# A seventh gate tile goes from the indexer to the selection, and each counting round hands out a larger share of stream work

## The chip, the cores and the metric

The kernel runs on one core of a Trainium2 chip. The metric is device time in microseconds (us). Three runs of the kernel before gave 1029.61, 1030.85 and 1031.7; the median is 1030.85. The engines are named as the profile names them: PE multiplies matrices (PEld loads its weights), ACT is ScalarE, DVE is VectorE, POOL is GpSimd, and SP issues most of the DMAs. SBUF is the on-chip memory, PSUM the small memory that PE writes its results to.

## The reference

One step of a one-layer encoder: 1024 prompt tokens and 32 sample tokens, model width 1024. A single projection yields everything that the branches need.

```python
h = rms_norm(x, g_norm) * (1.0 + scale) + shift
z = einsum('btd,de->bte', h, w_in)
u, zs, q, k, v, za, qi, ki, wi, gm = split(z, offs)

# indexer and selection
logits = einsum('bthd,bsd->bths', qi, ki) * IDX_DIM ** -0.5
score = einsum('bth,bths->bts', wi, relu(logits))     # -inf where not admissible
top_val, top_idx = top_k(score, n_sel)                # 256 (prompt), 136 (sample)
# attention over the selected keys only, then
ya = o * silu(za)
g_s, g_a = split(gm, 2)
merged = sigmoid(g_s) * (ys @ w_ps) + sigmoid(g_a) * (ya @ w_pa)
out = merged @ w_o
```

The gates gm have 2048 columns: 16 tiles of 128 columns, named g0 to g15 in the kernel. They are needed only at the end of the layer, so the kernel may compute them at any time after h.

## The kernel before

**Tiling.** The 1056 tokens lie in three blocks of 256, 384 and 416 columns (BW). A column tile of the projection is 128 columns of w_in: for each block and each of 8 slices of the model width, `mm3` (lines 271 to 273) issues three matmuls, since every operand is split into a high part and a low part (hH and hL, wh and wl). A tile is 72 matmuls. Its weights are loaded by SP (line 250), cast to wh on ACT (line 259) or POOL (263) and subtracted to wl on DVE or POOL (264). Each block ends with an evacuation of PSUM: for a gate tile a tanh on ACT (line 707); after the third block SP stores the tile (709).

**The stream.** Such tiles are jobs of a stream `Z` (class Stream). The other stages call `run(us)`: this writes as many matmuls of the stream into PE's program as make up that time (by a cost per step of 0.02 + 0.00132 times the block's columns; 11.65 us for a whole tile), between the matmuls of the stage itself. With the second step of a job's first block the next job's weights are split and those of the job after it loaded. With `Z.lag` a block's evacuation is written 4.5 us of handed-out work after its last matmul. PE, ACT and DVE execute in the order in which the program writes (manual schedule); POOL and SP are ordered by the scheduler.

**The stages around the change**, in order:

- The gated linear unit (glu), with qi1, the second pair of indexer heads, behind it in the stream.
- Key preparation: `run(KF)`, the cached keys turned (line 1185), the indexer's keys and weights turned (1194), kiH and kiL split (76 on DVE, 77 on POOL). Also a piece of the output gate (`rpiece`: a 1 MB load of rraw, and matmuls at line 1167).
- The indexer, four pairs of heads. For every pair (j) and every row tile i of 2 to 8, for both heads: score matmuls on PE (lines 1220, 1221), a ReLU on ACT (1223), scaling and sum on DVE (1226, 1228). Behind each, `run(0.25 + nk * FI)` hands out stream work. The score PSUM (pss) has two buffers.
- The selection: 32 counting rounds find each row's threshold bit by bit. In every round ACT counts four row tiles (line 1556), DVE three (1558); then `run(RS)` hands out stream work; then DVE makes the next threshold (1614, 1621). Then the mask stage ("mark"; lines 1628 to 1655), where `run` hands out by the tile's length, 45.2 us in all. Its stream: K, V and Q of the first head pair (K0, V0, Q0), the gate tiles from number NI to 15, four za tiles. In this stage a tile's first two blocks share one PSUM tile (pss, two buffers) and its third has one of another kind (pz, two buffers).
- The attention, with its own stream (K, V and Q of the next heads, then the tiles of w_ps).

The gate tiles are dealt out by two numbers: g0 to g(NS-1) go ahead of the indexer, up to g(NI-1) into the indexer, the rest into the selection.

```python
Z.add(qijob(1), *(gate_job(f, se, ve) for f in range(NS, NI - 1)))          # line 1135
Z.add(qijob(2), qijob(3), gate_job(NI - 1, se, ve), hold=True)
...
for b in range(31, -1, -1):
    ...
    for g in (B1, B2, A):
        g.count()
    run(RS)
    ve.tensor_tensor(keep, cnt, lim, op=ALU.is_ge)
```

qi2 is opened when pair 0 has been written, qi3 and the last gate tile when pair 1 has; so in pair 0 the stream holds what comes ahead of qi2.

Of the kernel before, what the change touches and what calls it, by code (L numbers as in the profile page):

```python
# [25 lines left out]
NCH = 133  # L26
NST = 134
QT = [(i * 128, 128, 128 * (i + 1)) for i in range(8)]
NS, NI = 6, 8
KF = 9.0  # L30
WB = 5
SQ, HF, SM, GD, GH, NP, BL, HB, GL = 1, 4, 4, (1, 1, 0), 1, (0, 0, 2, 2), 1, 1, 0
# [6 lines left out]
TF, TK, TW = 1.5, 1.0, 4.5  # L39
FI = 0.0006  # L40
KA, LA = 5.0, 1.0
LAG, RS, MS, RM, RB = 4.5, 4.1, 0.008, 14.0, 1
FA, FF, SW, SA, SB = ((2.0, 1.3), (2.0, 1.3), (2.4, 1.6), (1.5, 1.5)), 0.08, 1.2, 4.0, 1.0
YR = 3.9, 2.0, 2.0, 8.0, 3.0
MR, ML, YS, YW, HI, HG, JO, SF = (), 1, 10, 15, 0, 0, 8, (2, 2, 2, 1)
# [1876 lines left out]
```

## Time and profile before

| what | value |
|---|---|
| median of three runs | 1030.85 us |
| the profiled execution | 1031.07 us |
| its span, first to last instruction | 1029.3 us |
| busy: PE, PEld | 974.4 us (95%), 904.5 us (88%) |
| busy: DVE, ACT, POOL | 762.7 us (74%), 526.5 us (51%), 233.4 us (23%) |
| mean granted clock of PE | 0.989 |
| chain that ended last | PE 70%, ACT 9%, DVE 8%, DMA 6% |
| DMA, mean over the span | 121 GB/s |

Busy time is the time in which at least one instruction of the engine ran. Of the 40 slices of the page (25.7 us each), the indexer lies in the 12th to 15th, the selection in the 16th to 23rd. A row of the timeline reads: start in us, duration in us (ns in the groups), engine, source line, operation, output<-inputs, shape, and in brackets the engine's idle time ahead of it with the instruction that ended it. A wait for several things is put down to the one that came last by the profile, which can be wrong.

### The profile page before, as it was taken

What the parts mean: (1) busy time and instruction counts of PE and PEld (TensorE: products, weight loads), DVE (VectorE), ACT (ScalarE), POOL (GpSimd) and SP (SyncE); (2) the same over time, 40 slices, a digit from 0 to 9 for tenths busy, and PEclk for the clock granted to TensorE, in tenths of its full rate; (3) what the DMA queues carried; (4) which work ended last, traced back from release to release, by engine and by line L of the source; (5) the groups of instructions that cost most, each with busy time, mean ns of one, the idle gap of its engine ahead of it and who ended that gap; (6) DMA issues with size and microseconds to landing.
All of it is one profiled execution on the core that took longest, in us unless ns stands there. A gap on an engine that the chain in (4) does not pass through costs nothing.

```text
span 1029.3 us, 16904 instructions
## 1 busy us (share of the span) xinstructions
PE 974.4 (95%) x6034; PEld 904.5 (88%) x6034; DVE 762.7 (74%) x1743; ACT 526.5 (51%) x1126; POOL 233.4 (23%) x443
## 2 busy tenths in 40 slices
PE   5999999999999999989998999999999998999997
PEld 3789999999998889889998999999997997998786
DVE  4669899993866879899999758657557685886543
ACT  3642234435546666867994366466465554343111
POOL 3102400000010043333315423334311222530000
PEclk9999999999999999989998999999999999999999
DMA  9922524548483122323313422222416424653411
GB/s 318 277 78 84 147 74 120 128 98 260 134 260 103 40 83 83 93 65 106 102 63 105 136 85 63 88 79 63 132 56 205 131 64 151 209 171 118 133 62 61
DMA packets 134399, 124.24 MB, mean 121 GB/s; under 512 B 20400, under 2 KB 115076, under 8 KB 134316
## 3 DMA queue, kind: packets, MB, share of 16 engines
q1 hardware_dynamic: 133376, 122.62, 38.9%
q8 instruction: 47, 0.77, 0.3%
q10 hardware_dynamic: 780, 0.52, 0.2%
q14 instruction: 36, 0.29, 0.1%
q0 software_dynamic: 160, 0.03, 0.0%
HBM read 87.74 MB, written 34.83 MB: 119 GB/s over the span
## 4 chain that ended last, share of the span: by engine, by line
PE 70%; ACT 9%; DVE 8%; DMA 6%; issue 5%; POOL 1%; SPq 1%; POOLq 0%; ACTq 0%; DVEq 0%
PE pz L271 12%; PE pz L272 11%; PE pz L273 11%; ACT junkb L1556 5%; PE pss L1392 3%; PE psm L1891 3%; PE psm L1892 3%; PE psm L1893 3%; DMA wm<-in_w_mod 2%; PE pt L1485 2%; DVE junk L1558 2%; PE pspo L1504 2%; PE pss L271 2%; PE pss L273 2%; PE pss L272 2%
## 5 line engine op out<-in xcount | busy, mean ns | idle before, releaser
L271 PE MATMUL pz<-hH,wh 128*128 128x384 f32 (+4 forms) x760 | 259.9, 342 | 0.8 <-ACT tg L707 0.5
L272 PE MATMUL pz<-hL,wh 128*128 128x384 f32 (+4 forms) x760 | 250.4, 329 | 0.0
L273 PE MATMUL pz<-hH,wl 128*128 128x384 f32 (+4 forms) x760 | 250.3, 329 | 0.0
L264 POOL TENSOR_TENSOR wl<-raw,wh 128x256 fp32r<-128x256 f32 (+1 forms) x180 | 134.5, 777 | 105.5 <-ACT wh L259 105.2
L271 PEld LDWEIGHTS pz<-hH,wh 128*128 128x128 f32 (+1 forms) x760 | 143.1, 188 | 7.1 <-issue 3.0
L272 PEld LDWEIGHTS pz<-hL,wh 128*128 128x128 f32 (+1 forms) x760 | 142.5, 187 | 1.7
L273 PEld LDWEIGHTS pz<-hH,wl 128*128 128x128 f32 (+1 forms) x760 | 142.1, 187 | 1.3
L1556 ACT ACTIVATE junkb<-sco,thr 128x768 bf16<-128x768 f32 (+3 forms) x128 | 96.7, 756 | 32.0 <-DVE thr L1621 21.2
L1558 DVE TENSOR_SCALAR_CACHE_REDUCE junk<-sco,thr 128x1024 bf16<-128x1024 f32 (+2 forms) x96 | 105.4, 1098 | 2.2
L271 PE MATMUL pss<-hH,wh 128*128 128x256 f32 (+2 forms) x288 | 94.9, 329 | 7.7 <-POOL wl L264 4.1
L273 PE MATMUL pss<-hH,wl 128*128 128x256 f32 (+2 forms) x288 | 92.5, 321 | 2.4 <-POOL wl L264 2.4
L272 PE MATMUL pss<-hL,wh 128*128 128x256 f32 (+2 forms) x288 | 92.5, 321 | 0.0
L1488 DVE TENSOR_TENSOR PL<-pt,PH 128x512 fp32r<-128x512 f32 (+2 forms) x96 | 50.4, 552 | 34.4 <-ACT PH L1487 34.2
L263 POOL CAST wh<-raw 128x256 fp32r<-128x256 f32 x88 | 34.9, 437 | 175.7 <-PE pz L272 157.1
L271 PEld LDWEIGHTS pss<-hH,wh 128*128 128x128 f32 x288 | 57.3, 199 | 11.8 <-POOL wl L264 4.4
L1487 ACT CAST PH<-pt 128x512 fp32r<-128x512 f32 (+2 forms) x96 | 43.0, 483 | 46.4 <-PE pt L1485 45.2
L273 PEld LDWEIGHTS pss<-hH,wl 128*128 128x128 f32 x288 | 57.1, 198 | 3.1 <-POOL wl L264 3.1
L1228 DVE SCALAR_TENSOR_TENSOR sco<-rl,wi,sco 128x384 f32<-128x384 f32 (+6 forms) x49 | 46.9, 964 | 15.0 <-ACT rl L1223 13.9
L272 PEld LDWEIGHTS pss<-hL,wh 128*128 128x128 f32 x288 | 57.2, 199 | 0.3 <-DVE hL L77 0.2
L1223 ACT ACTIVATE rl<-pss 128x384 f32<-128x384 f32 (+6 forms) x56 | 40.9, 739 | 28.0 <-PE pss L1221 22.2
L1405 ACT ACTIVATE Sm<-Sm,mx 128x128 f32<-128x128 f32 (+8 forms) x68 | 52.7, 775 | 4.8 <-DVE mx L1398 4.4
L1893 PE MATMUL psm<-o,mL 128*128 128x512 f32 (+1 forms) x136 | 51.8, 381 | 0.0
(400 smaller groups left out, 2173.9 us busy)
## 6 DMA issues: line engine op xcount, KB each, us to landing
raw<-in_w_in SPq DMA_DIRECT2D x44, 512.0 KB
thD<-tg SPq DMA_DIRECT2D x16, 528.0 KB
tgl<-thD SPq DMA_DIRECT2D x16, 528.0 KB
wm<-in_w_mod SPq DMA_DIRECT2D x8, 1024.0 KB
rraw<-in_w_mod SPq DMA_DIRECT2D x4, 1024.0 KB
kd<-kd SPq DMA_DIRECT2D x32, 128.0 KB
xo<-in_x_prompt SPq DMA_DIRECT2D x8, 512.0 KB
rawo<-in_w_o SPq DMA_DIRECT2D x8, 512.0 KB
```

What stands on the lines that cost most here:

```text
L264: leng.tensor_sub(wl[:, c], raw[:, c], f32(wh[:, c]))
L271: te.matmul(ps, wh, xh, start=first, stop=False)
L272: te.matmul(ps, wh, xl, start=False, stop=False)
L273: te.matmul(ps, wl, xh, start=False, stop=last)
L1223: se.activation(rl[:m, :nk].rearrange("p (b c) -> p b c", c=w_), pv, AF.Relu)
L1228: ve.scalar_tensor_tensor(sco[i][:m, :nk], rl[:m, :nk], w, sco[i][:m, :nk], op0=ALU.mult, op1=ALU.add)
L1405: se.activation(P, P, AF.Exp, scale=-1.0, bias=self.mx, accum_out=self.rs)
L1487: se.copy(PH[:, b0:b1_, oc], src)
L1488: ve.tensor_sub(PL[:, b0:b1_, oc], src, f32(PH[:, b0:b1_, oc]))
L1556: se.activation(junkb[:m, :nk], x[:m], AF.Sign, bias=t, accum_out=cnt[:m, k:k + 1])
L1558: ve.tensor_scalar(junk[:m, :nk], x[:m], t, None, op0=ALU.is_lt, op1=ALU.add, accum_out=cnt[:m, k:k + 1])
L1893: te.matmul(ps, ml, wh, start=False, stop=last)
```

## The change

Two numbers change:

```diff
-NS, NI = 6, 8
+NS, NI = 6, 7
-LAG, RS, MS, RM, RB = 4.5, 4.1, 0.008, 14.0, 1
+LAG, RS, MS, RM, RB = 4.5, 4.6, 0.008, 14.0, 1
```

With NI = 7 the range NS to NI - 1 is empty: no gate tile stands between qi1 and qi2. g6 takes g7's place behind qi3, and g7 becomes a tile of the selection, behind Q0, where its weights are both cast and subtracted on POOL (before: cast on ACT, subtracted on DVE). With RS = 4.6 a counting round hands out 0.5 us more stream work, 147.2 us in 32 rounds instead of 131.2; the selection's stream has 16 tiles instead of 15. The attention's order on PE, DVE and ACT is the same but for a few evacuations and casts that move by a place or two.

On PE, ahead of head pair 0 of the indexer (pss the scores, pz the stream, hH and hL the split h, pt the turned keys, pg the output gate's piece), these rows stand before the change:

```order
L1167 MATMUL pg<-rraw,scP 32x512 x4
L271 MATMUL pz<-hH_81,wh 128x384
L272 MATMUL pz<-hL_83,wh 128x384
L273 MATMUL pz<-hH_81,wl 128x384
```

and at the first scores:

```order
L1220 MATMUL pss<-kiH,qis_2929 128x384
L1221 MATMUL pss<-kiL,qis_2929 128x384
L271 MATMUL pz<-hH_738,wh 128x416
L272 MATMUL pz<-hL_739,wh 128x416
L273 MATMUL pz<-hH_738,wl 128x416
L1220 MATMUL pss<-kiH,qis_2930 128x384
L1221 MATMUL pss<-kiL,qis_2930 128x384
```

and with the change the whole passage reads:

```order
L1185 MATMUL pt<-idf,cki 128x128 x4
L1194 MATMUL pt<-idf,zki 128x72 x8
L1194 MATMUL pt<-idf,zki 32x72
L1167 MATMUL pg<-rraw,scP 32x512 x4
L1220 MATMUL pss<-kiH,qis_2929 128x384
L1221 MATMUL pss<-kiL,qis_2929 128x384
L1220 MATMUL pss<-kiH,qis_2930 128x384
L1221 MATMUL pss<-kiL,qis_2930 128x384
L1220 MATMUL pss<-kiH,qis_2929 128x512
L1221 MATMUL pss<-kiL,qis_2929 128x512
```

All 72 matmuls of the tile are gone from here; pair 0's scores follow one another with no stream between them.

On ACT, at the last counting rounds (junkb the counts of the row tiles sco5, sco3, sco2, sco8; tg and zt the evacuations of the stream's tiles; wh_5667 the weights of za1; le the first row of the mask stage), before:

```order
L1556 ACTIVATE junkb_4231,cnt_4209<-sco5_3313,thr_4206 128x768
L1556 ACTIVATE junkb_4231,cnt_4209<-sco3_3311,thr_4206 128x512
L1556 ACTIVATE junkb_4231,cnt_4209<-sco2_3310,thr_4206 128x384
L1556 ACTIVATE junkb_4231,cnt_4209<-sco8_3316,thr_4206 32x544
L707 ACTIVATE tg_5537<-pss_5538 128x384
L259 CAST wh_5667<-raw_5555 128x1024
L1629 ACTIVATE junkb_4231,cnt_4209<-le_5700 128x1024
```

and with the change, where the same weights are wh_5661:

```order
L707 ACTIVATE tg_5532<-pss_5533 128x384
L259 CAST wh_5661<-raw_5550 128x1024
L1556 ACTIVATE junkb_4145,cnt_4123<-sco5_3313,thr_4120 128x768
L1556 ACTIVATE junkb_4145,cnt_4123<-sco3_3311,thr_4120 128x512
L1556 ACTIVATE junkb_4145,cnt_4123<-sco2_3310,thr_4120 128x384
L1556 ACTIVATE junkb_4145,cnt_4123<-sco8_3316,thr_4120 32x544
L707 ACTIVATE tg_5532<-pz_5617 128x416
L696 ACTIVATE zt_5653<-pss_5654 128x256
L1629 ACTIVATE junkb_4145,cnt_4123<-le_5733 128x1024
```

The cast of za1's weights has moved from behind the last round's counts to ahead of them.

On ACT, at the first gate tile of the selection (tg_4657 is g8 before; tg_4561 is g7 with the change, each the tile behind Q0), before:

```order
L1556 ACTIVATE junkb_4231,cnt_4209<-sco8_3316,thr_4206 32x544
L707 ACTIVATE tg_4657<-pss_4658 128x256
L1556 ACTIVATE junkb_4231,cnt_4209<-sco5_3313,thr_4206 128x768
L1556 ACTIVATE junkb_4231,cnt_4209<-sco3_3311,thr_4206 128x512
L1556 ACTIVATE junkb_4231,cnt_4209<-sco2_3310,thr_4206 128x384
L1556 ACTIVATE junkb_4231,cnt_4209<-sco8_3316,thr_4206 32x544
L707 ACTIVATE tg_4657<-pss_4658 128x384
```

and with the change:

```order
L1266 COPY tm_4474<-pt_4618 32x128
L1321 CAST qs0_4414<-pz_4510 64x384
L1321 CAST qs1_4415<-pz_4510 64x384
L1556 ACTIVATE junkb_4145,cnt_4123<-sco5_3313,thr_4120 128x768
L1556 ACTIVATE junkb_4145,cnt_4123<-sco3_3311,thr_4120 128x512
L1556 ACTIVATE junkb_4145,cnt_4123<-sco2_3310,thr_4120 128x384
L1556 ACTIVATE junkb_4145,cnt_4123<-sco8_3316,thr_4120 32x544
L707 ACTIVATE tg_4561<-pss_4562 128x256
L707 ACTIVATE tg_4561<-pss_4562 128x384
```

Before, the tile's second evacuation stands behind the counts of round 12 (the first behind those of round 11); now both stand behind the counts of round 10.

## The prediction

> **What bounds the kernel now.** I read first the busy time by stage, in the view of windows; the seven stretches are the end of the key preparation, head pair 0 of the indexer, pairs 1 to 3, the first and second half of the counting rounds, the mask stage, and the attention. Columns: length, then busy us (instructions) of PE, weight loads, DVE, ACT, POOL, then granted clock and DMA.
>
> ```profile
> 299.50:308.50 9.00, 9.00 (x68) 7.83 (x66) 6.06 (x6) 3.45 (x8) 3.56 (x1) 1.00 0.90 248
> 308.50:323.80 15.30, 14.00 (x74) 12.27 (x74) 9.81 (x13) 11.09 (x16) 0.00 (x0) 1.00 0.41 135
> 387.60:476.00 88.40, 82.14 (x508) 80.26 (x505) 80.10 (x177) 62.55 (x151) 28.22 (x53) 0.96 0.29 85
> 476.00:541.60 65.60, 62.76 (x384) 60.94 (x382) 61.49 (x143) 59.22 (x144) 16.95 (x32) 1.00 0.27 87
> 541.60:584.30 42.70, 39.10 (x226) 38.34 (x227) 40.95 (x60) 17.33 (x40) 20.93 (x23) 0.92 0.35 113
> 584.30:880.00 295.70, 283.36 (x1883) 265.24 (x1882) 193.04 (x554) 168.43 (x386) 87.95 (x186) 0.99 0.34 108
> ```
>
> In the attention PE is busy 283.36 of 295.70 us and DVE only 193.04: PE sets its length, so what starts it earlier ends the kernel earlier. In the selection (387.6 to 584.3) PE and DVE are both near full, so neither busy share decides; the waits do. PE's waits there, from the timeline of PE, between the start of the stage's first stream tile (387.55) and the attention's first scores (583.18), with one evacuation of ACT:
>
> ```profile
> 387.55 0.38 PE L271 MATMUL pss<-hH,wh 128*128 128x256 f32 x1
> 426.35 0.66 PE L1261 MATMUL pt<-idf,zf 128*128 128x128 f32 x4 [2.02 <-ACT tm L1263]
> 454.09 0.46 ACT L707 ACTIVATE tg<-pss 128x384 f32<-128x384 f32 x1
> 454.69 0.55 PE L271 MATMUL pss<-hH,wh 128*128 128x256 f32 x1 [4.05 <-POOL wl L264]
> 504.95 0.36 PE L271 MATMUL pss<-hH,wh 128*128 128x256 f32 x1 [0.80 <-ACT tg L707]
> 517.35 0.36 PE L271 MATMUL pss<-hH,wh 128*128 128x256 f32 x1 [0.74 <-POOL wh L263]
> 542.79 0.38 PE L271 MATMUL pss<-hH,wh 128*128 128x256 f32 x1 [1.24 <-ACT wh L259]
> 546.64 0.58 PE L273 MATMUL pss<-hH,wl 128*128 128x256 f32 x1 [1.70 <-POOL wl L264]
> 583.18 0.22 PE L1392 MATMUL pss<-kH,qs 128*128 128x128 f32 x1
> ```
>
> The waits stand at the starts of stream tiles, and mostly what is late is ScalarE: an evacuation (tg, L707) that frees PSUM, or the cast of the next weights (wh, L259). ScalarE does these between counting rounds, where the program put them; PE runs ahead of the rounds until no PSUM is free. (The 4.05 us is put down to POOL; I take it for the evacuation of g8's 384 block on ACT, whose row stands above it and ends at 454.55, as that frees the buffer this tile needs.) One tile without waits takes 11.66 us (504.95 to 517.35 less 0.74). Two waits cost more than themselves, by the windows of PE (length, busy, granted clock, DMA):
>
> ```profile
> 454.00:456.00 2.00, 1.31 (x6) 0.50 0.00 0
> 460.00:462.00 2.00, 2.00 (x13) 0.98 0.78 273
> 546.00:548.00 2.00, 1.36 (x6) 0.50 0.25 101
> ```
>
> After them the clock is 0.5 for some 6 us (in the first from before 454 to 460). DVE, in the same stage, has no such room. Its rows: round 1 (keep, L1614), rounds 7, 11, 17 and 18, round 32, the last mask piece, the first maxima of the attention, its scaling, and PE's first transposes of probabilities:
>
> ```profile
> 395.39 0.14 DVE L1614 TENSOR_TENSOR keep<-cnt,lim 128x7 int32<-128x7 f32 x1
> 421.81 0.17 DVE L1614 TENSOR_TENSOR keep<-cnt,lim 128x7 int32<-128x7 f32 x1
> 450.24 0.16 DVE L1614 TENSOR_TENSOR keep<-cnt,lim 128x7 int32<-128x7 f32 x1
> 479.06 0.17 DVE L1614 TENSOR_TENSOR keep<-cnt,lim 128x7 int32<-128x7 f32 x1
> 483.05 0.17 DVE L1614 TENSOR_TENSOR keep<-cnt,lim 128x7 int32<-128x7 f32 x1
> 541.52 0.17 DVE L1614 TENSOR_TENSOR keep<-cnt,lim 128x7 int32<-128x7 f32 x1
> 583.86 0.43 DVE L1637 TENSOR_TENSOR mb<-le,eq 32x544 bf16<-32x544 bf16 x1
> 584.32 0.29 DVE L1398 CUSTOM_DVE_ANT_0 Sm<-pss,mb 128x128 f32<-128x128 f32 x1
> 586.14 0.31 DVE L1414 TENSOR_SCALAR Sm<-Sm,rs 128x128 f32<-128x128 f32 x1
> 589.91 0.27 PE L1485 MATMUL pt<-idf,Sm 128*128 128x128 f32 x1
> ```
>
> A round is 3.99 us at its shortest (479.06 to 483.05) and 4.71 on average (146.1 us over 31). So **two chains end together** at 584: DVE's counts and masks, and PE's stream with its waits. Afterwards PE is the later one: the probabilities were ready at 586.45, PE came to them at 589.91.
>
> **The change, part by part.** *Indexer.* The slot of g6 leaves: 11.65 us of PE, a cast on ACT, a subtraction on DVE, three evacuations, a load and a store on SP's queue. It lay beside head pair 0:
>
> ```profile
> 299.48 0.36 PE L271 MATMUL pz<-hH,wh 128*128 128x256 f32 x1
> 304.07 3.56 POOL L77 TENSOR_TENSOR kiL<-kid,kiH 128x1568 fp32r<-128x1568 f32 x1 [12.71 <-DVE kiH L76]
> 308.50 0.34 PE L1220 MATMUL pss<-kiH,qis 128*128 128x384 f32 x1
> 309.09 0.48 ACT L1223 ACTIVATE rl<-pss 128x384 f32<-128x384 f32 x1
> 319.88 0.50 PE L1220 MATMUL pss<-kiH,qis 128*128 128x512 f32 x1 [0.86 <-ACT rl L1223]
> 322.18 0.31 PE L1220 MATMUL pss<-kiH,qis 128*32 128x272 f32 x1 [0.19 <-ACT rl L1223]
> 321.10 2.53 ACT L1223 ACTIVATE rl<-pss 128x1024 f32<-128x1024 f32 x3 [0.47 <-PE pss L1221]
> 323.63 0.33 PE L271 MATMUL pz<-hH,wh 128*128 128x384 f32 x1
> ```
>
> Pair 0 cannot start before kiL is done, 307.63; so it starts at 307.7 instead of 308.50, and of g6's place from 299.48 on nearly all becomes idle time of PE. From there its 14 tiles run bare. The last four do so already: two 1024 tiles take 2.30 us (319.88 to 322.18), 1.15 each, where PE has about 0.92 of work and ACT about 0.9 (2.53 us for two and a half). That is half of PE plus ACT, plus 0.2 of handing over. Over 14 tiles, 9,536 columns, PE has 8.6 us and ACT 9.0 (0.4 to 0.93 each), so 8.8 + 14 x 0.2 = 11.6, ending at 319.3 against 323.63: 4.3 gained. But PE was idle before, as ahead of 454.69; if its first 5 us go at half clock, about 1.4 is lost, and 2.9 remain. I take **3.7** of 11.65. Ends: all of pair 0 at half clock, 17.2 us, gives 324.9, 1.3 lost; ACT alone (9.0, begun 0.6 behind PE as at 309.09) gives 317.3, 6.3 gained.
>
> Beside that row, the Trainium skill ("TensorE: Matmul & The Clock Gate", Part 1, What's actually happening) says that the array falls to half clock after an idle window of about 3.4 us and recovers after about 3.4 us of sustained work. It speaks against this change, which makes such a gap; the trace agrees on the half (0.50) and shows longer, about 6 us, for the way back. By the rule's shorter time the loss would be about 1.0 instead of 1.4, an estimate from that page.
>
> *Selection, PE.* It gets a 16th tile: now it needs 195.7 (387.55 to 583.2): 15 tiles of 11.65, 12.7 idle by the three windows of the stage (6.26 + 2.84 + 3.60), about 5 of slow clock (some 5 us at half rate lose 2.5, twice), and 3.2 left for the transposes of K and V. With 16 tiles that is 189.6 and the waits. What remains of the waits: each round now hands out 4.6, so evacuations stand earlier among the rounds. A tile needs the PSUM of the tile but one before it; PE's lead over the work handed out may be 7 us (11.65 less a round) to 11.7 before it must wait. At 450.24, round 11, PE had done 57.5 (62.7 less 2.2 of waits and 3.0 of transposes) of 45.1 handed out: a lead of 12.4, hence the 4.05. With 4.6 a round and no earlier wait it is 59.7 - 50.6 = 9.1 there, 88.5 - 78.2 = 10.3 at 479.06, and then falls, as 15 rounds take 4.16 each: 3.8 at 541.52. So a tile may still wait a little between rounds 11 and 20: I keep 1.5 us of the 17.7. The cast for za1 stands a round before the end, not behind it: the waits from 542.79 to 546.64 go, with their slow clock. PE would end at 387.55 - 3.7 + 189.6 + 1.5 = 575.0, against 583.2. Ends: 573.5 with no wait, 591 with all of them kept.
>
> *Selection, DVE.* The same counts and masks; rounds with two tanh evacuations on ACT exist now as well. The store and the load of the tile go to SP's queue in the selection, under DMA shares of 0.27 to 0.35; uncovered they would show as the kd wait below. The added tile's split is now on POOL, beside DVE:
>
> ```profile
> 492.62 1.44 POOL L263 CAST wh<-raw 128x256 fp32r<-128x256 f32 x4 [8.04 <-PE pz L272]
> 495.99 0.17 DVE L1614 TENSOR_TENSOR keep<-cnt,lim 128x7 int32<-128x7 f32 x1
> 500.48 0.17 DVE L1614 TENSOR_TENSOR keep<-cnt,lim 128x7 int32<-128x7 f32 x1
> 464.24 0.43 DVE L76 CAST kH<-kd 128x512 fp32r<-128x512 f32 x1 [0.97 <-DMA kd<-kd]
> ```
>
> The round with such a split, 495.99 to 500.48, is 0.5 over 3.99; I allow 0.5 to 1.0. I add 0.7. The key splits (kH) come in rounds 10, 11, 12 instead of 11, 13, 14, so their reloads (SP's queue, kd) have one round less; one waited 0.97, and I add one such. DVE then ends at 584.3 - 3.7 + 0.7 + 1.0 = 582.3. Bounds: 580 (no additions) and 586 (two more kd waits and a contended copy of V).
>
> *Sum.* The transposes can begin 2.15 after the masks (586.45 - 584.3), at 584.45; PE, 6.7 us of other work after its stream's end (589.91 - 583.2), would be there at 581.7. DVE is the later: 589.91 - 584.45 = 5.5 us gained. Behind it nothing but PE's order counts, which is the same. The profiled execution took 1031.07, its span and 1.8 around it (the median shown is 1030.85): **1025.6**.
>
> **Rivals.** (a) *Nothing gained*: the gap PE gets in the indexer (11.65 - 3.7 = 8) is as large as the waits it loses later, if those fall from 17.7 only to about 8, as when the V and key work in rounds 9 to 12 stretches them again. Then PE ends at 581.5, comes to the transposes at 588.2, and the time is about 1029.4. For it: both engines are near full. Against: the lead. (b) *Slower*: the lead limit is hit as often as now, and the tile is simply added: 11.65 - 3.7 = 8 us late: 1039. It decides where the lead passes 12 us with 4.6 handed out, that is if rounds 7 to 16 take 2 us or more longer than today. Or the reverse, rounds waiting for PE at 4.6 each, cannot: at its smallest, 421.81, the lead is 34.3 - 2.2 - 32.2, about 0, and evacuations are put 4.5 behind the work they follow. (c) *More*: pair 0 at ACT's pace (6.3) and no additions on DVE: 589.91 - 578.0 - 2.15 = 9.8, 1021.3. (d) *The added split holds DVE whole*, for its 1.44 + 2.82 = 4.3 us instead of 0.7: DVE ends 3.6 later, 1029.2. Against it stands the row above with 0.5. The Trainium skill ("SBUF — State Buffer", Who interferes with whom) states such an exclusive hold of the ports that DVE and POOL share, for the whole of whichever instruction was issued first; the measured round decides against a hold of that length. (e) *The added hand-out does nothing*, as the stream would run out: 32 x 4.6 + 45.2 in the masks = 192.4 for 186.4 of tiles, 6 us of masks without stream; the time is DVE's anyway, and this is in the forecast.
>
> **How the numbers follow.** Forecast 0.62 with (e), own range 1022.5 to 1028.5; (a) 0.13; (b) 0.10; (c) 0.11; (d) 0.04. The range 1021 to 1031 takes in both ends of DVE's and of pair 0's cost, and leaves out (b), half of (c) and a little of (a). A measurement of this kernel tells about 0.2% (2 us) from no change. Faster 0.73 (forecast and (c)), same 0.17 ((a), (d)), slower 0.10 (b).
>
> **What the new profile would show.** Pair 0's first score at 307.7 and pair 1's stream at about 320, with PE's clock down near 305; no wait of 4 us at the start of a gate tile; the cast for za1 ahead of the last round; keep 31 rounds apart by about 147 us; PE's stream done several us before the last mask piece, which is near 582. Wrong it is if PE's end is later than the masks', or if the rounds grow beyond 150.

## The result, and the profile after

Four runs of the changed kernel gave 1019.49 to 1022.61 us, median **1022.2**, beside 1030.23 for the kernel before: a ratio of 0.9915 (95% interval 0.9893 to 0.9936). On a second chip it was 1020.06 against 1028.99, 0.9911 (0.9892 to 0.9930). The forecast was 1025.6, a gain of 5.5; it is 8.0. The time lies within the range of 1021 to 1031 that was stated, just below the 1022.5 to 1028.5 that were given to the forecast itself. The profiled execution took 1022.61, with a span of 1020.8 (before: 1031.07 and 1029.3).

In the traced execution of the changed kernel the stages ahead of the turned keys (L1185) happened to take 1.72 us longer, so I count from that row in every trace. First the rows of PE that start the stages (L1185, the output gate's piece, pair 0, the stream beside pair 1, K0):

```profile
300.85 0.60 PE L1185 MATMUL pt<-idf,cki 128*128 128x128 f32 x4
306.97 1.94 PE L1167 MATMUL pg<-rraw,scP 128*32 128x512 f32 x8 [2.83 <-DMA rraw<-in_w_mod]
308.83 0.69 PE L1220 MATMUL pss<-kiH,qis 128*128 128x384 f32 x1
321.69 0.34 PE L271 MATMUL pz<-hH,wh 128*128 128x384 f32 x1
382.91 0.36 PE L271 MATMUL pss<-hH,wh 128*128 128x256 f32 x1
```

DVE's rounds 1, 17, 18 and 32, its last mask piece, the first maxima and their scaling:

```profile
391.38 0.15 DVE L1614 TENSOR_TENSOR keep<-cnt,lim 128x7 int32<-128x7 f32 x1
466.73 0.17 DVE L1614 TENSOR_TENSOR keep<-cnt,lim 128x7 int32<-128x7 f32 x1
470.75 0.18 DVE L1614 TENSOR_TENSOR keep<-cnt,lim 128x7 int32<-128x7 f32 x1
539.23 0.17 DVE L1614 TENSOR_TENSOR keep<-cnt,lim 128x7 int32<-128x7 f32 x1 [0.77 <-ACT junkb L1556]
582.09 0.43 DVE L1637 TENSOR_TENSOR mb<-le,eq 32x544 bf16<-32x544 bf16 x1
582.55 0.29 DVE L1398 CUSTOM_DVE_ANT_0 Sm<-pss,mb 128x128 f32<-128x128 f32 x1
583.61 0.29 DVE L1414 TENSOR_SCALAR Sm<-Sm,rs 128x128 f32<-128x128 f32 x1
```

PE's larger waits from K0 on to the transposes (before: 12.7 us idle, 10.6 of it in the six waits shown with the prediction, up to 4.05):

```profile
424.89 0.29 PE L1261 MATMUL pt<-idf,zf 128*32 128x128 f32 x1 [0.60 <-ACT kall L1349]
452.89 0.46 PE L271 MATMUL pz<-hH,wh 128*128 128x416 f32 x1 [1.98 <-ACT tg L707]
493.17 0.36 PE L271 MATMUL pss<-hH,wh 128*128 128x256 f32 x1 [0.47 <-ACT tg L707]
575.79 0.33 PE L1392 MATMUL pss<-kH,qs 128*128 128x128 f32 x1 [1.63 <-ACT zt L696]
579.87 0.45 PE L271 MATMUL pz<-hH,wh 128*128 128x384 f32 x1 [0.61 <-ACT zt L696]
583.95 0.33 PE L1485 MATMUL pt<-idf,Sm 128*128 128x128 f32 x1 [0.33 <-DVE Sm L1414]
```

And the stages by windows (length, then busy us of PE, weight loads, DVE, ACT, POOL, then clock and DMA): the key preparation, pair 0, the rounds in two parts, the masks, the attention.

```profile
301.20:308.80 7.60, 2.87 (x20) 0.98 (x18) 3.55 (x6) 3.09 (x7) 3.33 (x1) 0.75 0.92 261
308.80:321.70 12.90, 11.76 (x53) 8.48 (x50) 8.49 (x12) 9.24 (x13) 0.17 (x1) 0.88 0.29 91
382.90:473.00 90.10, 87.40 (x555) 85.89 (x556) 81.87 (x177) 63.52 (x154) 33.66 (x61) 1.00 0.31 92
473.00:539.30 66.30, 65.83 (x405) 65.37 (x404) 61.71 (x143) 60.26 (x146) 20.50 (x38) 1.00 0.28 89
539.30:582.50 43.20, 40.96 (x261) 40.34 (x260) 41.62 (x60) 16.86 (x38) 23.68 (x26) 1.00 0.38 125
582.50:878.20 295.70, 284.23 (x1888) 266.96 (x1887) 199.06 (x565) 168.52 (x388) 86.08 (x182) 0.99 0.35 110
```

The idle time of PE has moved to the key preparation (4.7 of 7.6 us), as foreseen; in the selection it is busy for 194.2 of 199.6 us and its clock stays at 1.00, where it was 0.96 and 0.92 in two of these stages. The first transposes now wait for DVE (0.33 for Sm), so DVE is the later one, but only just. (Of the 4.05 us wait of before, which the profile put down to POOL, the prediction said that it was for ACT's evacuation. In e11, a run of the same program up to there, the profile puts the wait of 4.01 at this place down to ACT tg L707.)

The same points in us behind L1185, from the timelines of before and after and of three experiments (c1 is the changed kernel again, e1 the tile moved without the larger hand-out, e2 the hand-out without the tile):

| point | before | after | c1 | e1 | e2 |
|---|---|---|---|---|---|
| pair 0's first score | 9.37 | 7.98 | 8.33 | 8.22 | 10.15 |
| stream beside pair 1 | 24.50 | 20.84 | 20.70 | 20.74 | 25.27 |
| last score of pair 3 | 87.09 | 81.60 | 81.44 | 81.47 | 86.33 |
| round 1 | 96.26 | 90.53 | 90.37 | 90.40 | 95.50 |
| round 32 | 242.39 | 238.38 | 238.34 | 236.71 | 242.96 |
| end of the last mask piece | 285.16 | 281.67 | 281.65 | 278.63 | 284.31 |
| first transposes | 290.78 | 283.10 | 283.09 | 289.61 | 285.74 |
| end of the span | 730.17 | 719.95 | 718.72 | 728.01 | 724.00 |

7.7 us are gained up to the transposes (forecast 5.5) and 2.5 behind them (forecast none); the 1.72 that the early stages lost come off.

### The profile page after: what moved, and what is told of

Its sections match the earlier page's. It is cut to its first block, busy times and chain, and to the rows that moved or that the text cites. A ratio compares the mean times of both kernels' runs of the same rounds, so it can differ in the third digit from the quotient of the medians.

```text
span 1020.8 us, 16910 instructions
## 1 busy us (share of the span) xinstructions
PE 970.2 (95%) x6034; PEld 901.6 (88%) x6034; DVE 762.4 (75%) x1742; ACT 525.1 (51%) x1125; POOL 240.7 (24%) x451
## 4 chain that ended last, share of the span: by engine, by line
PE 49%; DVE 14%; ACT 11%; issue 4%; DMA 2%; POOL 0%; POOLq 0%; ACTq 0%; DVEq 0%; SPq 0%
PE pz L271 8%; PE pz L272 7%; PE pz L273 7%; ACT junkb L1556 7%; DVE junk L1558 3%; PE pss L1392 3%; PE psm L1891 3%; PE psm L1892 3%; PE psm L1893 3%; PE pt L1485 2%; PE pspo L1504 2%; PE pspo L1502 2%; PE psm L273 2%; PE psm L272 2%; PE pss L1220 2%
## 5 line engine op out<-in xcount | busy, mean ns | idle before, releaser
L271 PE MATMUL pz<-hH,wh 128*128 128x384 f32 (+4 forms) x744 | 254.3, 342 | 2.9 <-ACT tg L707 2.0
L272 PE MATMUL pz<-hL,wh 128*128 128x384 f32 (+4 forms) x744 | 245.3, 330 | 0.0
L273 PE MATMUL pz<-hH,wl 128*128 128x384 f32 (+4 forms) x744 | 245.3, 330 | 0.0
L264 POOL TENSOR_TENSOR wl<-raw,wh 128x256 fp32r<-128x256 f32 (+1 forms) x184 | 137.8, 779 | 101.2 <-ACT wh L259 100.9
L271 PEld LDWEIGHTS pz<-hH,wh 128*128 128x128 f32 (+1 forms) x744 | 139.9, 188 | 7.5 <-ACT tg L707 2.3
L272 PEld LDWEIGHTS pz<-hL,wh 128*128 128x128 f32 (+1 forms) x744 | 139.2, 187 | 1.6
L273 PEld LDWEIGHTS pz<-hH,wl 128*128 128x128 f32 (+1 forms) x744 | 138.9, 187 | 1.4
L272 PE MATMUL pss<-hL,wh 128*128 128x256 f32 (+2 forms) x304 | 95.7, 315 | 0.0
L273 PE MATMUL pss<-hH,wl 128*128 128x256 f32 (+2 forms) x304 | 95.5, 314 | 0.0
L263 POOL CAST wh<-raw 128x256 fp32r<-128x256 f32 x92 | 39.1, 466 | 168.5 <-PE pz L272 151.8
L1228 DVE SCALAR_TENSOR_TENSOR sco<-rl,wi,sco 128x384 f32<-128x384 f32 (+6 forms) x49 | 46.8, 960 | 12.4 <-ACT rl L1223 11.1
```

The source lines that it names most:

```text
L264: leng.tensor_sub(wl[:, c], raw[:, c], f32(wh[:, c]))
L271: te.matmul(ps, wh, xh, start=first, stop=False)
L272: te.matmul(ps, wh, xl, start=False, stop=False)
L273: te.matmul(ps, wl, xh, start=False, stop=last)
L1228: ve.scalar_tensor_tensor(sco[i][:m, :nk], rl[:m, :nk], w, sco[i][:m, :nk], op0=ALU.mult, op1=ALU.add)
```

## The experiments

Three chips were used, each with its own runs of the kernel before; a ratio is always to those.

| run | median us | before | ratio (95%) |
|---|---|---|---|
| e1_tile_only | 1029.88 | 1029.25 | 1.0014 (1.0000 to 1.0028) |
| e2_handout_only | 1026.50 | 1029.25 | 0.9980 (0.9967 to 0.9992) |
| e3_dve_plus | 1027.71 | 1029.25 | 0.9981 (0.9967 to 0.9996) |
| e4_kil_early | 1026.33 | 1029.25 | 0.9974 (0.9961 to 0.9988) |
| c1_changed_again | 1020.06 | 1028.99 | 0.9911 (0.9892 to 0.9930) |
| e5_before_dve_plus | 1032.08 | 1028.99 | 1.0028 (1.0014 to 1.0042) |
| e6_kil_first_piece | 1022.55 | 1028.99 | 0.9931 (0.9912 to 0.9950) |
| e7_rounds_uneven | 1026.96 | 1028.99 | 0.9977 (0.9963 to 0.9992) |
| e9_warm | 1022.43 | 1030.11 | 0.9919 (0.9899 to 0.9940) |
| e10_warm_kil | 1022.25 | 1030.11 | 0.9926 (0.9906 to 0.9945) |
| e11_before_credit | 1027.49 | 1030.11 | 0.9974 (0.9958 to 0.9990) |
| e12_after_credit | 1023.10 | 1030.11 | 0.9932 (0.9911 to 0.9953) |

### The two halves alone

The changed kernel with the old hand-out (e1):

```diff
-LAG, RS, MS, RM, RB = 4.5, 4.6, 0.008, 14.0, 1
+LAG, RS, MS, RM, RB = 4.5, 4.1, 0.008, 14.0, 1
```

> The tile is moved (NI = 7), the hand-out stays at 4.1. Theory (the two parts need each other: DVE's chain starts earlier through the shorter head pair 0, but PE's stream has to be done with it): 32 x 4.1 + 45.2 = 176.4 us are handed out for 186.4 of tiles, so 10 us of stream are left behind the last mask piece, and PE waits between rounds 9 and 20 as before the change. Transposes about 6 us later than before the change: 1036 us (1033 to 1040). Rival (the shorter pair 0 alone makes the gain): 1025 or less.

The changed kernel with the old place of g6 and g7 (e2):

```diff
-NS, NI = 6, 7
+NS, NI = 6, 8
```

> Only the hand-out is raised to 4.6, g6 stays beside head pair 0 (NI = 8). Theory (DVE sets the end of the selection once PE's waits are gone): DVE's rounds and masks end where they did, PE is no longer late, so that the transposes come 3.5 us earlier and no more (589.91 to 586.45): 1026.7 us (1025 to 1029). Rival 1 (the whole gain is the removed PE waits): 1022. Rival 2 (the hand-out alone does nothing): 1030.

> The changed kernel once more, unaltered, beside the kernel before and the next three on one chip: what they are to be compared with. 7 to 8 us under the kernel before (0.991 to 0.994), transposes 283 us behind the turned keys of L1185.

The tile alone gains nothing (1.0014), the hand-out alone 0.2%, both together 0.9%. The table of points says why. In e1 DVE's masks end 6.5 us earlier than before, but the transposes come 11.0 us behind them: PE has a tile more and comes late. In e2 DVE's chain stands where it was and PE is early; its first transposes wait (the first row from the timeline of e2, the second a window of its PE: length, busy, instructions, clock, DMA):

```profile
586.24 0.47 PE L1485 MATMUL pt<-idf,Sm 128*128 128x128 f32 x1 [8.66 <-DVE Sm L1414]
587.00:589.00 2.00, 2.00 (x8) 0.50 0.00 1
```

That is the theory's picture for e2, and its time is 1026.5 against 1026.7 forecast. For e1 both expectations missed: 1029.9, not 1036 and not 1025. Its PE starts K0 81.93 us behind L1185 (before: 88.42), 6.5 earlier, and its waits in the stage sum to 8.5 us by its timeline instead of 12.7; 11.65 - 6.5 - 4.2, and 2 less of slow clock, is the -1.2 that its transposes show. My expectation had kept all of the old waits.

### Who ends the selection

```diff
         mark(B)
+    for _ in range(4):
+        dz = sel.tile([128, 1024], F32, name="low")
+        ve.tensor_tensor(dz, sco[7], sco[7], op=ALU.add)
```

The same lines went into the changed kernel (e3) and into the kernel before (e5).

> The changed kernel with four more additions of 128x1024 on DVE (results unused) between the last mask piece and the attention's first maxima, some 4.5 us. Theory (DVE sets the end of the selection): all of it shows, 1022.2 + 4.3 = 1026.5 us (1025.5 to 1027.5). Rival (PE's stream and first scores set it, DVE has room): 1.5 or less, 1022 to 1023.7.

> The kernel before with the same four additions on DVE ahead of the attention (4.9 us), which cost the changed kernel 5.05 us up to the transposes. Theory (before the change PE was the later one by 3.5 to 4.2 us, so DVE had that much room): 0.7 to 1.4 us, 1.0007 to 1.0015 of the kernel before. Rival (DVE set the end before, too): 4.5 to 5 us, 1.0045 or more.

DVE's added rows and PE's first transposes, with a PE window behind them, e3 first, then the two rows of e5:

```profile
580.89 4.99 DVE L1659 TENSOR_TENSOR low<-sco 128x1024 f32<-128x1024 f32 x4
587.42 0.47 PE L1485 MATMUL pt<-idf,Sm 128*128 128x128 f32 x1 [5.35 <-DVE Sm L1414]
588.00:590.00 2.00, 2.00 (x7) 0.50 0.00 0
```

```profile
583.02 5.56 DVE L1659 TENSOR_TENSOR low<-sco 128x1024 f32<-128x1024 f32 x4
590.27 0.33 PE L1485 MATMUL pt<-idf,Sm 128*128 128x128 f32 x1 [2.56 <-DVE Sm L1414]
```

In e3 the transposes come 288.15 us behind L1185, 5.05 later than in the changed kernel: all of the 4.99 arrives. The time rises by more, 0.9981 against 0.9911 (7 us): behind the wait of 5.35 PE's clock is 0.50 for over 4 us. In e5, of 5.56 us 2.56 arrive and 3.0 were room, near the 3.5 that the prediction read; the time rises by 3.1, between what theory and rival gave. So PE was the later one before and DVE is now.

### Starting pair 0 earlier

```diff
-    split(kiH, kiL, kid, ve, ge)
+    for c, eng in ((slice(0, 512), ve), (slice(512, 1568), ge)):
+        split(kiH[:, c], kiL[:, c], kid[:, c], ve, eng)
```

with RM 20 for all four pieces of the output gate (e4), or 3 us more for the first alone (e6). The expectation of e6 says that the other pieces stay where they were. They do not, since each piece starts the next one: in e6 the four stand 8.9, 33.3, 61.8 and 82.6 us behind L1185, in c1 6.5, 26.6, 54.3 and 80.2.

> The changed kernel with kiH and kiL made in two pieces, columns 0 to 511 both on DVE, the rest of kiL on POOL, and the output gate's piece 6 us later (RM 20), so that pair 0 need neither wait for the whole of kiL (ends 308.97) nor for the load of rraw (306.97). Theory (what starts pair 0 earlier moves DVE's chain through rounds and masks, and PE has 2.6 us of room at the transposes): pair 0's first score about 2 us earlier, 1020.2 us (1019.5 to 1021.5). Rival (gains before the counting rounds are lost in them or at PE): 1022.

> As the run with early kiL, but the output gate's pieces stay where they were save the first, whose matmuls come 3 us later (behind three score tiles of pair 0), so that the last piece's load cannot hold up K0. Theory (there PE waited 5.57 us for that load ahead of K0, ACT then for K0's matmuls, and DVE 8.1 us for ACT's counts in the rounds; without it the 3.9 us that pair 0 begins earlier are kept): first score 4 us, round 1 some 4.5 us, transposes 3.5 to 4 us earlier than in the changed kernel, which makes the time 3.5 us less. Rival (the rounds give back whatever DVE wins ahead of them, since PE's stream does not start earlier): time of the changed kernel, within 1 us.

e4's first score came 4.05 us behind L1185 and round 1 85.99 (c1: 8.33 and 90.37), but the transposes 4.3 later than in c1. Its rows, one line number higher; the last two are from the views of waits (total, times, longest) of DVE and ACT in the rounds:

```profile
388.68 1.94 PE L1167 MATMUL pg<-rraw,scP 128*32 128x512 f32 x8 [5.56 <-DMA rraw<-in_w_mod]
DVE keep L1615 <- ACT junkb L1557: 8.1, 4, 2.9
ACT zf L1306 <- PE pss L273: 5.2, 1, 5.2
```

The last piece's load came late, PE waited ahead of K0, ACT for K0, and DVE for ACT's counts: the rounds took 156.8 us instead of 147.97. Here the rounds do wait for PE. e6 is free of that wait, and still gains nothing: pair 0 begins at 5.11 instead of 8.33, the stream beside pair 1 at 20.58 instead of 20.70. I suspected PE's clock. e9 (in the changed kernel) and e10 (in e6) put transposes into PE's two gaps; e10 has 10 in place of the 18:

```diff
+        if k == 3:
+            for _ in range(10):
+                te.transpose(pt[:, 288:416], cki[:, 0].rearrange("p a d -> p (a d)"), idf)
         if k % 4 == 3 or k == 8:
...
+    pt = ps_t()
+    for _ in range(18):
+        te.transpose(pt[:, 0:128], cki[:, 0].rearrange("p a d -> p (a d)"), idf)
```

> The changed kernel with 28 more transposes on PE whose results are unused, 10 in the 1.9 us wait ahead of the second group of L1194 and 18 in the 2.95 us wait ahead of the output gate's piece (0.15 us each), so that PE is busy in the gap that the moved tile left. Theory (that gap halves PE's clock from 303 to 309, which costs 0.9 us in the piece and 1.4 us in pair 0's first scores): granted clock 1.00 there, the piece 1.07 instead of 1.94, pair 1's stream 18.4 us behind L1185 instead of 20.7, time 2.3 us less than the changed kernel, 0.989 of the kernel before. Rival (the half clock is hidden by ACT's ReLUs or lost again in the rounds): 0.991.

> The run with kiL in two pieces and the first piece of the output gate behind three score tiles, with 20 unused transposes in PE's two gaps. Theory (its earlier start of pair 0, 5.1 instead of 8.3 us behind L1185, was lost since these scores ran at half clock until 311): at full clock pair 1's stream begins 17.6 us behind L1185 instead of 20.6, the time is about 3 us under the changed kernel, 0.988. Rival (pair 0 is set by something else, kiL's second piece on POOL or ACT): 20 or more behind L1185, 0.991 to 0.993.

PE's windows of 1 us in the changed kernel, where the low clock begins and ends, then one of 2 us in e9; the start of the stream beside pair 1 in e6 and in e10; and in e9 the second matmul of pair 0 with what it waits for:

```profile
304.00:305.00 1.00, 0.14 (x3) 0.98 1.03 399
305.00:306.00 1.00, 0.00 (x0) 0.50 1.07 393
311.00:312.00 1.00, 1.00 (x4) 0.60 1.01 377
312.00:313.00 1.00, 0.90 (x6) 1.00 1.06 412
306.00:308.00 2.00, 1.58 (x16) 1.00 1.01 384
320.85 0.33 PE L271 MATMUL pz<-hH,wh 128*128 128x384 f32 x1
317.71 0.33 PE L271 MATMUL pz<-hH,wh 128*128 128x384 f32 x1
311.30 0.44 PE L1227 MATMUL pss<-kiL,qis 128*128 128x384 f32 x1 [0.60 <-POOL kiL L77]
```

With the unused transposes the clock stays at 1.00 and the piece takes 1.06 instead of 1.94. Alone that is worth 0.5 us at pair 1 (20.18 against 20.70), since pair 0 then waits for kiL, which is there 8.1 to 8.3 behind L1185 in both kernels. With kiL early it is worth 2.2 (18.36 in e10 against 20.58 in e6). But of the 2.3 us by which e10 leads c1 there, 1.4 are left at the last score of pair 3, 1.2 at round 1, 0.4 at round 32 and 0.6 at the transposes; nothing shows in the time. So both rivals hold in part.

Where the lead is lost can be read from the points. From the last score of pair 2 to that of pair 3 it is 1.1 us longer in e6 and e10 than in c1, and one of the output gate's pieces (1.06 us) then still lies ahead of K0; in c1 it lies within pair 3. These are the two runs in which the pieces were moved by 3 us and more, a likely reason. And in the three runs in which round 1 and K0 move apart, round 32 goes with K0: against c1, round 1, K0 and round 32 stand at -4.4, +5.8 and +4.5 us in e4, at +1.0, +1.7 and +1.5 in e6, and at -1.2, -0.5 and -0.4 in e10. So by these three runs an earlier round 1 is worth little or nothing as long as PE does not come to K0 earlier as well. Which of K0's results the rounds then wait for is shown only for e4.

### The rounds

```diff
-        run(RS)
+        run(4.1 if b > 23 else 4.77)
```

> The changed kernel with 4.1 us handed out in the first eight rounds and 4.77 in the other 24 (147.3 in all, as now). Theory (4.6 in the early rounds writes stream evacuations on ACT ahead of counts before PE has done their matmuls, so the rounds wait for PE: 31 rounds take 147.85 with 4.6 and 146.3 with 4.1, tile moved or not): the 31 rounds take about 146.4, the time is 1.3 us less than that of the changed kernel. Rival (the longer rounds come from the added evacuations and POOL's splits themselves): 147.8, no change.

The 31 rounds take 148.4 us, not 146.4, so the theory's sum falls. That the early rounds never wait for PE does not follow from it. In e7 DVE's waits for the casts of Q0 (qs) are back at the 3.8 us that they take with 4.1 (4.4 in the changed kernel); that much of the theory holds. What is lost is lost later: e1 and e7 hand out 4.1 in the first eight rounds and need 39.3 and 39.4 us from round 1 to round 9, but from there to round 32 it is 107.0 us in e1, with 4.1, and 109.1 in e7, with 4.77. What DVE waits for in the rounds are ACT's counts and casts (changed kernel, two rows; then e2 and e1 for the counts):

```profile
DVE qs L1325 <- ACT qs L1321: 4.4, 3, 1.9
DVE keep L1614 <- ACT junkb L1556: 1.2, 2, 0.8
DVE keep L1614 <- ACT junkb L1556: 2.1, 4, 0.8
DVE keep L1614 <- ACT junkb L1556: 0.2, 1, 0.2
```

The time rose by 7 us against the changed kernel. 1.7 of it stand at the transposes; behind them its trace needs 439.1 us instead of 435.6 (c1), with a wait of 3.26 instead of 1.88 for the cached keys and a slow clock after it. The order of PE's work behind the transposes is another one too, so this stretch does not speak of the rounds:

```profile
741.95 0.44 PE L1348 MATMUL pt<-idf,ckt 128*128 128x128 f32 x1 [3.26 <-DMA ckt<-in_cache_k]
```

Together that is 5.1 us. The rest is not in the trace: the traced execution took 1024.68 us, 2.3 less than the median.

### Behind the transposes

The stream keeps a credit of time not yet handed out. At the end of the masks it is 0.178 in the kernel before and 0.239 in the changed one; this alone changes the order of the attention on PE. By the rows of the traces, ten steps of the stream (three matmuls each) stand one place earlier with the change, and at two places transposes of probabilities come later. (The expectation below counts eight.)

```diff
     Z.until("za3")
     Z.flush()
+    Z.credit += 0.061
```

This is e11, in the kernel before; e12 takes 0.061 off in the changed kernel. Behind the transposes PE's rows of e11 are then those of the changed kernel, one for one, and those of e12 are those of the kernel before.

> The kernel before, with 0.061 us added to the stream's credit at the end of the masks (0.178 before, 0.239 in the changed kernel): the attention's PE program is then that of the changed kernel, eight stream steps a place earlier, and all ahead of it stays. Theory (the waits of PE at the m evacuations of L1590 are shorter in that order: the stretch from the last transposes of L1485 to the end is 162 to 163 us with NI 8 and 161 in the changed kernel): 161 there, 1.4 to 2 us less in all, 0.998 to 0.9986 of the kernel before. Rival (the difference behind the transposes was chance): 163, 1.000.

> The reverse: the changed kernel with 0.061 us taken from the stream's credit at the end of the masks, so that its attention has the PE program of the kernel before. Theory: 162 to 163 us from the last transposes of L1485 to the end, 1.4 to 2 us more than the changed kernel, 0.9925 to 0.993. Rival (chance): 161, 0.991.

e11 is at 0.9974, 2.6 us faster than the kernel before (1.0 to 4.3 by its interval). e12 is at 0.9932; the changed kernel was at 0.9915 and 0.9911 in its own runs and, with the unused transposes, at 0.9919 on e12's chip (e9). That is the direction of the theory, but the intervals overlap, and 1.3 us of it stand in e12's trace ahead of the edit (first transposes 284.40 us behind L1185, against 283.09 in c1). So the traces have to tell. From the first transposes to the end they take 439.4, 439.5 and 438.0 us in the order of before (before, e5, e12), and 436.9, 435.6 and 435.3 in the other (after, c1, e11). Slow clock is little of that: before and after lose 1.7 each to it, and the other four have none there. So the order is worth 2.4 us by e12 and c1.

The mechanism that I expected is not what the traces show: from the last transposes to the end e11 takes 161.5 and e12 161.8 us, and the large waits for m evacuations are the same in both orders. Two smaller waits go with the order. They stand in the traces of before, e5 and e12, and in none of after, c1, e4, e6, e9, e10 and e11 (a row of before for the first, then before and e12 for the second):

```profile
617.10 1.09 PE L1485 MATMUL pt<-idf,Sm 128*128 128x128 f32 x8 [0.45 <-ACT Sm L1412]
816.50 0.45 PE L271 MATMUL pz<-b,wh 128*128 128x384 f32 x1 [0.59 <-DVE m L1590]
809.94 0.44 PE L271 MATMUL pz<-b,wh 128*128 128x384 f32 x1 [0.59 <-DVE m L1590]
```

With the first the transposes behind it come 0.5 us later; the second makes 0.8 us between two m evacuations (14.0 us in before and e12, 13.2 in c1 and e11). What the other 1.1 us are isn't shown, and single traces differ by as much: e10, which has the changed order, takes 438.4 us, 1.7 of it slow clock.

## Why the prediction was right, and where it was off

**Two chains that end together.** Right. e5 shows the room that DVE had before (3.0 us; 3.5 read from the rows), e2 and e3 that DVE sets the end once PE's waits are gone. What the prediction did not see is that DVE's rounds hang in turn on PE's start of K0, plainly in e4 and by differences of less than 1 us in e6 and e10.

**Indexer, 3.7 of 11.65.** Right: 3.66 and 3.80 in the two traces (24.50 to 20.84 and 20.70). But the prediction had worked out 4.3 at full clock and 2.9 with the half clock, and took a number between them without a reason, so that it came out is in part luck. Pair 0 began 8.0 to 8.3 us behind L1185, held by the piece and kiL together (forecast: 8.6), and ran 12.4 to 12.9 us (11.6 at full clock, 13.0 with the half clock). The half clock came as foreseen, from 305 to 311.6, of which PE worked 4.6 us (from 306.97; the sum had 5); but its price of 1.4 was too high by 0.9, since kiL would hold pair 0 anyway (e9), and the bare pace too short by 0.3 (8.3 to 20.18 at full clock, 11.9 instead of 11.6).

What was not in the sum: round 1 came 5.7 us earlier, not 3.7. In the traced execution of before, pair 2 took 22.2 us with PE's clock at 0.5 for some 3 us; it took 20.6 to 20.7 without that in e2, e5 and the changed kernel (and 22.2 again in e11). That is 1.5 us in the trace from which I summed, and among traces of the old order it is chance: before and e11 have it, e5 and e2 do not. Whether the change has a part in it is open: with the tile moved, PE's wait ahead of this stretch is 1.06 us instead of 1.49, and none of the ten traces has slow clock in pair 2. Another 0.4 is pair 1's.

**Selection, PE.** The 4.05 us wait and those at 542 to 547 are gone, with their slow clock. 3.05 us of waits remain up to the stream's end (0.60, 1.98, 0.47; forecast 1.5), the largest between rounds 11 and 12, where the lead was said to be near its limit, and 1.63 ahead of the attention's first scores. PE begins these 274.9 us behind L1185; the forecast was 275.9, by a start of K0 2.7 us too late and waits that were too small.

**Selection, DVE.** The size was right, the reasons were not. The rounds take 147.85 us, 1.7 more than before, as summed (0.7 for POOL's split, 1.0 for a wait for kd). But no kd wait is in the changed kernel's trace. e1, which has the split, takes 146.31 for its rounds and e2, which has the hand-out, 147.46, against 146.13: the split costs about 0.2, the hand-out 1.3, as ACT's counts end later in rounds that carry more evacuations ahead of them (1.2 us of waits for junkb, of which the kernel before lists none, and 4.4 instead of 3.8 for qs). Rounds with two evacuations were named in the prediction, and given no price. The mask stage is 0.5 longer (43.3 against 42.8); with one half of the change it is 41.9 (e1) and 41.4 (e2). The traces show what both together lengthen: the last mask piece takes 4.8 us instead of 3.6, since POOL now splits weights beside it. The first two instructions of that piece and POOL's subtraction in the changed kernel, then the same two in e1, where POOL is idle:

```profile
577.73 0.85 DVE L1628 TENSOR_SCALAR le<-sco,thr 32x544 bf16<-32x544 f32 x1
578.51 0.96 DVE L1631 TENSOR_SCALAR eq<-sco,thr 32x544 bf16<-32x544 f32 x1
576.35 3.71 POOL L264 TENSOR_TENSOR wl<-raw,wh 128x256 fp32r<-128x256 f32 x4
574.18 0.49 DVE L1628 TENSOR_SCALAR le<-sco,thr 32x544 bf16<-32x544 f32 x1
574.60 0.49 DVE L1631 TENSOR_SCALAR eq<-sco,thr 32x544 bf16<-32x544 f32 x1
```

**The sum.** From the last mask piece to the transposes it is 1.43, not 2.15, since the first maxima are scaled 1.06 us after they begin (582.55 to 583.61), and before 1.82. With 5.7 instead of 3.7 at round 1, 1.7 lost in the rounds, 0.5 in the masks and 0.7 gained here, DVE's chain is 2.2 us earlier than forecast: 7.7 instead of 5.5. "Behind it nothing but PE's order counts, which is the same" was **the step that failed**, and so was the sentence on the attention's order ahead of the prediction: ten stream steps had moved on PE. By the times of e11 that is worth 2.6 us, by the traces of e12 and c1 2.4; 2.5 were gained there and none was forecast.

**The rivals.** (a) and (b) did not happen, but e1 shows how close (a) stood: with 4.1 handed out, the gap in the indexer and the tile eat all that DVE gains. (d) is refuted as a price: e1's rounds are 0.2 us longer, not 3.6. But the hold is in the traces. The instructions on 128x7 that make the next threshold (keep, thr, nxt) take 0.17 us alone and up to 0.70 beside a subtraction of POOL (mostly 0.74 each), while DVE's counts of 1.27 us keep their length beside the same subtractions. Over the 31 rounds what they take above 0.17 adds up to 5.3 us in e2 and 7.2 in the changed kernel, 6.0 in before and 9.2 in e1. Why the rounds grow by so much less isn't shown; DVE's waits are 1.0 to 1.1 us shorter in the kernels with the added split. (c) gave the nearer time, 1021.3, by a mechanism that did not happen: pair 0 gained 3.7, not 6.3. Against (b) I had written that rounds cannot wait for PE; e4 shows that they do when K0 starts behind round 1 (1.7 us there, against 8.5 ahead of it in c1).

## What to carry to other kernels

Where two engines end a stage together, a change that helps one and a change that helps the other may each show nothing or little alone (here 1.0014 and 0.9980) and pay when they are made together (0.991). Work that fills a gap gives back only a part of its price when it is taken out, if what remains there is paced by another engine: here 3.7 of 11.65 us. When a budget is changed, compare the whole order behind it too: a remainder of 0.06 us in a scheduler's credit moved steps up to 240 us later.

## What the runs showed that I had not expected

A wait of PE costs again afterwards. When PE took up work again behind waits of 4.05 (before), 5.35 (e3) and 8.66 us (e2), and behind the pair of 1.89 and 2.83 ahead of pair 0, the granted clock stayed at 0.50 for another 4 to 6 us; behind the 1.98 and 1.63 us in the changed kernel's trace it was 1.00. Between these it is chance: in c1, the same kernel, the wait that is 1.98 in that trace is 1.97 us, ends at 451.54, and the clock falls to 0.50 behind it. Ahead of pair 2 of the indexer, the kernel before and e5 both wait 1.49 us for the same ReLU. A window of c1, then the same 1 us of PE, 2 to 3 us behind the wait for the ReLU, in before and in e5:

```profile
454.00:456.00 2.00, 2.00 (x7) 0.50 1.03 295
345.00:346.00 1.00, 1.00 (x5) 0.50 0.70 210
345.00:346.00 1.00, 1.00 (x8) 1.00 0.83 249
```

Such a stretch costs 1.5 to 3 us (busy time times what the clock lacks of 1, summed over windows of 2 us from L1185 on), and which of them occur differs between executions: the sum is 8.7 us in the trace of the kernel before, 7.2 in e11 and 5.0 in e5, which run the same program up to the end of the masks, and 1.7 to 6.9 in the eleven others. So a forecast summed from one trace takes in a few us of chance, and it is a likely reason why single runs of the kernel before lie up to 6.6 us apart on one chip. Of the 75 runs of it beside the experiments, the 18 with a mean granted clock of 0.985 or less have a median of 1031.6 us, the 27 with 0.992 or more 1028.4.
